# Six merged-head operands loaded ahead of the last projection rows, two of them through ScalarE's queue, and the first dense product written ahead of later casts

## The chip, the cores and the metric

The kernel runs on one core of one Trainium2 chip. Its engines are TensorE (PE, with PEld for its weight loads), VectorE (DVE), ScalarE (ACT), GpSimd (POOL) and SyncE (SP); the last does nothing here but issue DMAs. The metric is the device time of one execution in microseconds, given as the median of the runs.

## The reference

One layer of a streaming encoder on a sequence of 2048 tokens of 1024 features: an attention sub-layer with two groups of eight heads, an output projection of the merged heads, and a squared-ReLU MLP.

```python
def reference(x, c, g_norm1, w_in, g_q, g_k, rel_bias, w_o, g_norm2, w1, w2, w_ada, b_ada):
    ...
        mod = c_act @ w_ada[l] + b_ada[l]
        sh1, sc1, gt1, sh2, sc2, gt2 = [m[:, None, :] for m in jnp.split(mod, 6, axis=-1)]
        h = rmsnorm(x, g_norm1[l]) * (1.0 + sc1) + sh1
        proj = h @ w_in[l]
        q_sb, k_sb, v_sb, q_ca, k_ca, v_ca = jnp.split(proj, split_pts, axis=-1)
        ...
        o_sb = stick_breaking_attention(...)
        ...
        o_ca = chunked_relpos_attention(q_ca, k_ca, hs(v_ca, N_CA_HEADS), rel_bias[l])
        mixed = jnp.concatenate([o_sb.reshape(B, S, D_SB), o_ca.reshape(B, S, D_CA)], axis=-1)
        x = x + gt1 * (mixed @ w_o[l])
        h = rmsnorm(x, g_norm2[l]) * (1.0 + sc2) + sh2
        x = x + gt2 * (jnp.square(jax.nn.relu(h @ w1[l])) @ w2[l])
```

## The kernel before, in words

Everything is computed in float32 by splitting each operand into a high and a low part and multiplying three times (high by high, high by low, low by high): `mm3`. Activations lie transposed, features on the 128 partitions, tokens along the free axis. The tokens are cut into four blocks of 512; the program calls them g or tb, 0 to 3.

The program has four stages. The first projects the input. The second is the attention, head by head, with the remaining projections put between its matmuls. The third is the seam that the change touches. The fourth is the MLP, whose two products are taken apart into seven smaller ones each (the numbers 1, 5, 6, 3, 7, 2, 4 in names such as `ps_0_5` and `opw_0_6`).

At the seam stand, in this order on PE:

- `po_4` to `po_7`: the last four of the eight output projections of token block 1. Each is 24 matmuls of 128x512, of a weight tile `ow_n` (1 MB, one DMA) and eight operands `fx`. The function `row()` writes one of them.
- `pso_5`, `pso_6`, `pso_7`, `pso_0` to `pso_4`: the eight output projections of token block 0 (class `Mixed`), again 24 matmuls each. Their moving operands are `opm_0` to `opm_7`, the merged heads of block 0, loaded by `Mixed.fetch` with eight DMAs of 512 KB from the scratch tensors `scr_m`. `pso_5` to `pso_7` keep the weight tiles `ow_5` to `ow_7` of the rows before; the others have their own, `wo_n`.
- the first dense products of the MLP (class `First`): `ps_0_1`, `ps_0_5`, then those that are added on top in a second PSUM bank, `ps_s`. That bank first gets a copy of `ps_0_1`, made by ACT (`ps_0_1_s`).

The scratch tensors `scr_m_0` to `scr_m_3` of block 0 are stored by SP well before. `scr_m_4` to `scr_m_6` are stored by POOL's queue and `scr_m_7` by ACT's queue; the last three of these come out of the last heads of the attention, while PE is already at `po_4`.

While PE is at the seam, DVE and ACT normalize and split the inputs of the MLP, one of four groups at a time. The first group is loaded into four tiles `ty`, the others into `cy`; `some(k, n)` writes stage n of group k. `txr_n` and `cxr_n` are the residual rows, added by DVE to the finished projections.

What sets the order: each engine executes its instructions in the order in which they stand in the program, a DMA-issuing instruction among them. The recording layer adds the waits. A DMA issued by SP or ACT takes one of eight completion counters, DMAHW0 to DMAHW7, one after the other over both queues, and waits until the DMA that had this counter before it has landed. POOL's DMAs have counters of their own, DMASW0 and so on.

Of the kernel before, what the change touches and what calls it, by code (L numbers as in the profile page):

```python
# [9 lines left out]
F32 = mybir.dt.float32  # L10
# [14 lines left out]
KT = D // P  # L25
# [54 lines left out]
def encoder_kernel(ctx, tc, xs, c, g1, g2, w_in, w_first, w_rest, gqk, bias, w_o, w1, w2, w_ada, b_ada, out):  # L80
    nc = tc.nc
    act, dve, pool, sp = nc.scalar, nc.vector, nc.gpsimd, nc.sync
# [20 lines left out]
    def scratch(name, shape, *counts):  # L103
        return {i: dram.tile(shape, F32, name=name + "_".join(map(str, i))) for i in product(*map(range, counts))}
# [4 lines left out]
    scr_m = scratch("scr_m", [P, 2, TB], NTB, KT)  # L109
# [134 lines left out]
    if True:  # L244
# [251 lines left out]
        act, dve, pool = (Ordered(tc, e) for e in (act, dve, pool))  # L496
# [58 lines left out]
        for i, e in ((0, dve), (KT // 2, pool)):  # L555
            ks = slice(i, i + KT // 2)
# [101 lines left out]
        sp = osp  # L658
# [78 lines left out]
    if True:  # L737
# [7 lines left out]
        sp = nc.sync  # L745
# [262 lines left out]
        class Filler:  # L1008
# [7 lines left out]
            def fetch(self, n):  # L1016

                while len(self.tiles) < n:
                    pl = (hx2, hxp, hxp)[turn[0] % 3]
                    turn[0] += 1  # L1020
                    for k in range(len(self.tiles), len(self.tiles) + KT // 2):
                        t = pl.tile([P, 2, TB], F32R, tag="hx", name=f"fx{turn[0]}_{k}")
                        sp.dma_start(t.bitcast(F32), self.src(k))
                        self.tiles.append(t)
# [332 lines left out]
        steps = [(u, st) for u in units for st in range(STEPS)]  # L1357

        turns = {STEPS * n: 4 if u.ca else 8 for n, u in enumerate(units) if n and u.ca != units[n - 1].ca}
        for i in range(len(steps) + LAG):  # L1360
# [31 lines left out]
            n = len(urgent) + len(heavy)  # L1392
# [14 lines left out]
    sp = osp  # L1407
# [21 lines left out]
    if True:  # L1429
# [35 lines left out]
        steps, jobs = [], {}  # L1465
# [510 lines left out]
        class Mixed(Step):  # L1976
# [6 lines left out]
                self.tiles = 0 if at else KT  # L1983
                self.frees = KT if at == KT - 1 else 0

            def fetch(self, *ks):
                for k in range(*ks):
                    m = Mixed.parts[k] = opp.tile([P, 2, TB], F32R, tag="op", name=f"opm{self.g}_{k}")
                    sp.dma_start(m.bitcast(F32), scr_m[self.g, k])

            def load(self):
                g, n = self.g, self.n
# [98 lines left out]
        def some(k, *ns):  # L2091
            for n in ns:
                blocks[k][n]()
# [3 lines left out]
        def row():  # L2097

            while force(left) is False:
                pass  # L2100
            while len(stores) > 2:
                stores.pop(0)()
            return force(left)

        steps[0].fetch(0, KT // 2)
        row()
        row()
        some(0, 0)
        steps[0].fetch(KT // 2, KT - 2)
        row()  # L2110
        some(0, 1)
        steps[0].fetch(KT - 2, KT)
        row()
        some(0, 2)
        some(1, 0)
# [15 lines left out]
        ahead = iter(steps[1:])  # L2131
        nxt = next(ahead)
        for n, s in enumerate(steps):
            while nxt is not None and ready - used + nxt.tiles <= 8 and nxt.ready():
                nxt.prepare()
                ready += nxt.tiles
                nxt = next(ahead, None)
            for m in (0, 1) if n == 0 else (n + 1,):
                if m < KT:
                    steps[m].load_row()  # L2140
            for job in jobs.get(n, ()):
                job()
            if n == KT - 1:
                firsts = spare.tile([P, 2, 2, TB], F32R, tag="r8", name="opr")
                steps[KT].prepare(firsts[:, 0])
                steps[KT].fetch(0)
                steps[KT + 1].prepare(firsts[:, 1])
                for m in range(1, 4):
                    steps[KT].fetch(m)
            s.run()  # L2150
            used += s.frees
            later.tick()
        later.flush()
# [42 lines left out]
```

## Time and profile before

| | us |
|---|---|
| median of 3 runs | 2514.77 (2513.28 to 2515.25) |
| profiled execution, its time | 2516.38 |
| profiled execution, span of the trace | 2514.6 |
| PE busy | 2498.9 (99%) |
| DVE busy | 2027.7 (81%) |
| ACT busy | 1526.4 (61%) |
| POOL busy | 787.1 (31%) |
| mean granted clock of PE | 0.999 |

The page gives each engine's busy time, and the span in 40 slices of 62.9 us. The timeline lists instructions in order of time, neighbours of a kind merged: start, length, engine, line, operation, output<-inputs, shape, count, and in brackets the idle time ahead of the first with what ended it. Nearly every instruction is recorded by a helper at line 42, so names of tiles tell them apart. SPq and ACTq are the issuing of DMAs; how long one takes to land stands in the answers on a tile.

### The profile page before, as it was taken

The numbers are of one execution on the slowest core, as the hardware profiler recorded it, in microseconds if no ns is written. First come the engines' busy times: TensorE is split into PE (matmuls) and PEld (weight loads), VectorE is DVE, ScalarE is ACT, GpSimd is POOL, SyncE is SP. The second block draws the span as 40 slices with busy tenths as digits, with TensorE's granted clock in tenths as the row PEclk, the third lists the DMA queues.
The fourth block names the chain that finished last, engine by engine and source line by source line (L and its number), as shares of the span: only waits on it lengthen the run. The fifth ranks groups of instructions, "written<-read, shape, count | busy, mean of one in ns | idle before, by whom it ended". The sixth has DMA issues, their size and how long they took to land.

```text
span 2514.6 us, 39505 instructions
## 1 busy us (share of the span) xinstructions
PE 2498.9 (99%) x12364; PEld 2094.8 (83%) x12364; DVE 2027.7 (81%) x3567; ACT 1526.4 (61%) x2928; POOL 787.1 (31%) x1174
## 2 busy tenths in 40 slices
PE   9999999999999999999999999999999999999999
PEld 8888888888888888888888888888888888888887
DVE  7656777897799888999858777779877759799998
ACT  6333424778876686666755555567555546577765
POOL 4330154777776677776710000000000000010100
PEclk9999999999999999999999999999999999999999
DMA  9879978789888788866786878996998996888982
GB/s 357 333 297 362 356 269 291 233 262 311 268 262 260 237 259 254 268 195 216 213 323 245 299 285 305 330 351 191 327 323 269 315 363 262 320 249 282 303 280 84
DMA packets 295970, 704.71 MB, mean 280 GB/s; under 512 B 32080, under 2 KB 88400, under 8 KB 284112
## 3 DMA queue, kind: packets, MB, share of 16 engines
q1 hardware_dynamic: 287552, 684.35, 79.3%
q0 software_dynamic: 6768, 13.11, 2.9%
q10 hardware_dynamic: 1440, 4.72, 0.5%
q8 instruction: 98, 1.61, 0.3%
q14 instruction: 112, 0.92, 0.1%
HBM read 473.99 MB, written 228.07 MB: 279 GB/s over the span
## 4 chain that ended last, share of the span: by engine, by line
PE 86%; DVE 5%; DMA 4%; ACT 2%; issue 1%; POOL 0%; SPq 0%; DVEq 0%; ACTq 0%; POOLq 0%
PE ps L42 24%; PE ps_s L42 15%; PE pt L42 11%; PE acc L42 7%; PE wt L42 7%; PE pf L42 6%; PE z L42 5%; PE po L42 4%; PE pq L42 3%; PE cz L42 2%; PE ct L42 1%; DMA scr_t<-twn 1%; DMA hw<-in_w_dram 1%; DVE h L42 1%; DMA opm<-scr_m 1%
## 5 line engine op out<-in xcount | busy, mean ns | idle before, releaser
L42 ACT CAST wth<-wt 128x512 fp32r<-128x512 f32 (+3 forms) x544 | 257.5, 484 | 173.3 <-PE wt L42 160.7
L42 PE MATMUL ps<-h,opw 128*128 128x512 f32 x1512 | 358.6, 389 | 0.0
L42 POOL TENSOR_TENSOR b<-p 128x512 f32<-128x512 f32 (+1 forms) x320 | 291.9, 912 | 155.7 <-DVE p L42 95.6
L42 DVE TENSOR_TENSOR wtl<-wt,wth 128x512 fp32r<-128x512 f32 (+3 forms) x544 | 291.2, 547 | 60.7 <-ACT wth L42 56.2
L42 PEld LDWEIGHTS ps<-h,opw 128*128 128x128 f32 x1512 | 283.6, 188 | 58.9
L42 PE MATMUL pt<-w,ht 128*128 128x512 f32 x1248 | 288.0, 391 | 0.0
L42 PE MATMUL ps_s<-h,opw 128*128 128x512 f32 x1152 | 277.6, 390 | 1.5 <-ACT ps_s L42 1.0
L42 PEld LDWEIGHTS pt<-w,ht 128*128 128x128 f32 x1248 | 232.9, 188 | 47.5
L42 DVE TENSOR_TENSOR_SCAN p<-z,p,zero 128x512 f32<-128x512 f32 x192 | 245.3, 1279 | 20.6 <-ACT z L42 14.9
L42 PEld LDWEIGHTS ps_s<-h,opw 128*128 128x128 f32 x1152 | 215.7, 188 | 47.9 <-ACT ps_s L42 1.4
L42 ACT CAST opr<-r 128x512 fp32r<-128x512 f32 x280 | 174.3, 623 | 118.2 <-PE ps L42 65.6
L42 PE MATMUL acc<-wth,v 128*128 128x512 f32 (+3 forms) x544 | 221.3, 410 | 1.1 <-ACT o L42 1.1
L42 PE MATMUL ps<-opr,ol 128*128 128x512 f32 x960 | 220.3, 389 | 0.0
L42 PEld LDWEIGHTS ps<-opr,ol 128*128 128x128 f32 x960 | 180.1, 188 | 37.8 <-DVE opr L42 0.4
L42 ACT ACTIVATE z<-z 128x512 f32<-128x512 f32 (+1 forms) x320 | 166.6, 521 | 54.3 <-PE z L42 49.9
L42 DVE TENSOR_TENSOR opr<-r,opr 128x512 fp32r<-128x512 f32 x280 | 185.7, 684 | 13.7 <-ACT opr L42 12.5
L42 PE MATMUL acc<-wtl,v 128*128 128x512 f32 (+3 forms) x544 | 185.6, 347 | 0.0
L42 PE MATMUL z<-k,q 128*128 128x512 f32 (+3 forms) x640 | 182.8, 367 | 1.0 <-DVE p L42 0.9
L42 POOL DMA_DIRECT2D scr_x<-txu x12 | 10.4, 866 | 547.7 <-ACT txu L42 545.9
L42 PE MATMUL ps<-oph,opv 128*128 128x512 f32 x768 | 175.7, 390 | 1.2 <-DVE oph L42 0.9
L42 PE MATMUL wt<-ident,b 128*128 128x128 f32 x1088 | 170.7, 272 | 0.4 <-DVE p L42 0.4
L42 PEld LDWEIGHTS ps<-oph,opv 128*128 128x128 f32 x768 | 143.9, 188 | 32.6 <-DVE oph L42 1.4
(238 smaller groups left out, 5062.1 us busy)
## 6 DMA issues: line engine op xcount, KB each, us to landing
r<-scr_hid SPq DMA_DIRECT2D x80, 512.0 KB, 7.4
q<-scr_q SPq DMA_DIRECT2D x128, 256.0 KB, 5.2
w<-in_w_dram SPq DMA_DIRECT2D x64, 512.0 KB, 5.7
k<-scr_k SPq DMA_DIRECT2D x240, 128.0 KB, 4.6
v<-scr_v SPq DMA_DIRECT2D x120, 256.0 KB, 4.6
wa<-in_w_ada_dram SPq DMA_DIRECT2D x48, 512.0 KB, 6.3
ow<-scr_wo SPq DMA_DIRECT2D x24, 1024.0 KB, 6.7
l<-scr_t SPq DMA_DIRECT2D x20, 1024.0 KB, 8.6
```

The lines of the kernel that those rows point to most:

```text
L42: return lambda *x, **y: self.tc.keep_in_program_order(f(*x, **y))
```

## The change

Three things move; no work is added or taken away.

1. Before, `opm_0` to `opm_3` were fetched ahead of the first row, `opm_4` and `opm_5` behind the second and the `ty` loads, `opm_6` and `opm_7` behind the third. Now `opm_0` to `opm_5` are fetched on SP and `opm_6`, `opm_7` on ACT, all ahead of the first row.
2. `Mixed.fetch` has a parameter for the queue.
3. The product `ps_0_1` (step number KT of the list) is written at the top of its turn, ahead of the preparation of the next five operands, and not behind it.

```diff
-            def fetch(self, *ks):
+            def fetch(self, *ks, queue=sp):
                 for k in range(*ks):
                     m = Mixed.parts[k] = opp.tile([P, 2, TB], F32R, tag="op", name=f"opm{self.g}_{k}")
-                    sp.dma_start(m.bitcast(F32), scr_m[self.g, k])
+                    queue.dma_start(m.bitcast(F32), scr_m[self.g, k])
...
-        steps[0].fetch(0, KT // 2)
+        steps[0].fetch(0, KT - 2)
+        steps[0].fetch(KT - 2, KT, queue=act)
         row()
         row()
         some(0, 0)
-        steps[0].fetch(KT // 2, KT - 2)
         row()
         some(0, 1)
-        steps[0].fetch(KT - 2, KT)
         row()
         some(0, 2)
         some(1, 0)
...
         for n, s in enumerate(steps):
+            if n == KT:
+                s.run()
             while nxt is not None and ready - used + nxt.tiles <= 8 and nxt.ready():
                 nxt.prepare()
...
-            s.run()
+            if n != KT:
+                s.run()
```

The order of PE's and DVE's instructions stays as it was. SP's queue at the seam, with the counters that each DMA waits for. Before:

```order
L42 DMA opm_3_16965<-scr_m_3_163 128x1024 [waits DMAHW4_49]
L42 DMA ow_6_16968<-scr_wo_236 128x2048 [waits DMAHW5_49,PE_49]
L42 DMA txr_5_16970<-in_xs_dram 128x512 [waits DMAHW6_49,Pool_49]
L42 DMA ow_7_16998<-scr_wo_237 128x2048 [waits DMAHW7_49,PE_49]
L42 DMA txr_6_17000<-in_xs_dram 128x512 [waits DMAHW0_49]
L42 DMA ty_0_11_17004<-scr_x_0_216 128x512 [waits DMAHW1_49]
L42 DMA ty_0_12_17006<-scr_x_0_208 128x512 [waits DMAHW2_49]
L42 DMA ty_0_21_17008<-scr_x_4_220 128x512 [waits DMAHW3_49]
L42 DMA ty_0_22_17010<-scr_x_4_212 128x512 [waits DMAHW4_49]
L42 DMA opm_4_17012<-scr_m_4_164 128x1024 [waits DMAHW5_49,DMASW0_49]
L42 DMA opm_5_17014<-scr_m_5_165 128x1024 [waits DMAHW6_49,DMASW1_49]
```

And with the change, the same stretch of SP's queue:

```order
L42 DMA opm_3_16965<-scr_m_3_163 128x1024 [waits DMAHW4_49]
L42 DMA opm_4_16967<-scr_m_4_164 128x1024 [waits DMAHW5_49,DMASW0_49]
L42 DMA opm_5_16969<-scr_m_5_165 128x1024 [waits DMAHW6_49,DMASW1_49]
L42 DMA ow_6_16976<-scr_wo_236 128x2048 [waits DMAHW0_49,PE_49]
L42 DMA txr_5_16978<-in_xs_dram 128x512 [waits DMAHW2_49,Pool_49]
L42 DMA ow_7_17006<-scr_wo_237 128x2048 [waits DMAHW3_49,PE_49]
L42 DMA txr_6_17008<-in_xs_dram 128x512 [waits DMAHW4_49]
L42 DMA ty_0_11_17012<-scr_x_0_216 128x512 [waits DMAHW5_49]
L42 DMA ty_0_12_17014<-scr_x_0_208 128x512 [waits DMAHW6_49]
L42 DMA ty_0_21_17016<-scr_x_4_220 128x512 [waits DMAHW7_49]
L42 DMA ty_0_22_17018<-scr_x_4_212 128x512 [waits DMAHW0_49]
```

`opm_4` and `opm_5` moved ahead of the weights `ow_6` and `ow_7`, and with them the counters moved: the DMA that waits for counter 0 was `txr_6` and is now `ow_6`.

ACT's queue at the end of the attention. Before, the store of the last merged heads, which takes counter 0, is followed by the first group of the MLP's inputs:

```order
L42 DMA scr_m_7_167<-os_7_0_16719 128x1024 [waits DMAHW0_49,Pool_49]
L42 ACTIVATE ty_0_11_17004<-ty_0_11_17004,mod,aff 128x512 [waits DVE_49]
L42 ACTIVATE ty_0_12_17006<-ty_0_12_17006,mod,aff 128x512 [waits DVE_49]
L42 ACTIVATE ty_0_21_17008<-ty_0_21_17008,mod,aff 128x512 [waits DVE_49]
L42 ACTIVATE ty_0_22_17010<-ty_0_22_17010,mod,aff 128x512 [waits DVE_49]
```

With the change, two loads stand between them:

```order
L42 DMA scr_m_7_167<-os_7_0_16719 128x1024 [waits DMAHW0_49,Pool_49]
L42 DMA opm_6_16971<-scr_m_6_166 128x1024 [waits DMAHW5_49,DMAHW3_49,DMAHW6_49,DMAHW2_49,DMAHW7_49,DMAHW1_49,DMASW2_49]
L42 DMA opm_7_16973<-scr_m_7_167 128x1024 [waits DMAHW1_49,DMAHW0_49]
L42 ACTIVATE ty_0_11_17012<-ty_0_11_17012,mod,aff 128x512 [waits DVE_49]
L42 ACTIVATE ty_0_12_17014<-ty_0_12_17014,mod,aff 128x512 [waits DVE_49]
```

`opm_6` waits for POOL's store of `scr_m_6` (DMASW2), `opm_7` for ACT's own store of `scr_m_7` (DMAHW0) to land.

ACT again, at the first dense products (`opw` are casts of the MLP's weights). Before:

```order
L42 CAST opr<-ts_0_1_5_17488 128x512 [waits DVE_49]
L42 CAST opw_0_6_17524<-ts_0_1_6_17492 128x512 [waits DMAHW1_49,DVE_49,PE_49]
L42 CAST opw_0_3_17527<-ts_0_1_3_17494 128x512 [waits DMAHW2_49,DVE_49,PE_49]
L42 CAST opw_0_7_17530<-w_1_0_17441 128x512 [waits DMAHW4_49,DVE_49,PE_49]
L42 CAST opw_0_2_17533<-w_1_0_17441 128x512 [waits PE_49]
L42 CAST opw_0_4_17536<-w_1_0_17441 128x512 [waits DMAHW5_49,PE_49]
L42 COPY ps_0_1_s<-ps_0_1_17539 128x512 [waits PE_49]
```

With the change:

```order
L42 CAST opr<-ts_0_1_5_17488 128x512 [waits DVE_49]
L42 COPY ps_0_1_s<-ps_0_1_17524 128x512 [waits PE_49]
L42 CAST opw_0_6_17539<-ts_0_1_6_17492 128x512 [waits DVE_49]
L42 CAST opw_0_3_17542<-ts_0_1_3_17494 128x512 [waits DMAHW2_49,DVE_49]
L42 CAST opw_0_7_17545<-w_1_0_17441 128x512 [waits DMAHW4_49,DVE_49]
L42 CAST opw_0_2_17548<-w_1_0_17441 128x512
L42 CAST opw_0_4_17551<-w_1_0_17441 128x512 [waits DMAHW5_49]
```

The copy into the second bank moved ahead of the five casts.

## The prediction

> **What bounds the kernel now.** The page comes first.
>
> ```profile
> PE 2498.9 (99%) x12364; PEld 2094.8 (83%) x12364; DVE 2027.7 (81%) x3567; ACT 1526.4 (61%) x2928; POOL 787.1 (31%) x1174
> ```
>
> PE is busy for 99% of the span, so the kernel can gain only where PE stands still, and loses wherever PE is made to stand. The change touches one stretch of about 80 us, so the second view is PE's timeline there.
>
> ```profile
> 1268.66 22.00 PE L42 MATMUL po<-fx,ow 128*128 128x512 f32 x96
> 1290.50 4.29 PE L42 MATMUL pso<-opm,ow 128*128 128x512 f32 x18
> 1296.38 0.96 PE L42 MATMUL pso<-opm,ow 128*128 128x512 f32 x3 [1.59 <-DMA opm<-scr_m]
> 1297.63 11.86 PE L42 MATMUL pso<-opm,ow 128*128 128x512 f32 x51 [0.29 <-DMA opm<-scr_m]
> 1309.33 27.36 PE L42 MATMUL pso<-opm,wo 128*128 128x512 f32 x120
> 1336.53 5.81 PE L42 MATMUL ps<-h,opr 128*128 128x512 f32 x24
> 1343.30 3.04 PE L42 MATMUL ps_s<-h,opw 128*128 128x512 f32 x12 [0.96 <-ACT ps_s L42]
> ```
>
> PE stands still three times: 1.59 and 0.29 us for the late operands opm_6 and opm_7, and 0.96 us for ACT's copy into the second bank. Together 2.84 us, or 0.11% of the run: all that the change can win here. Where it can lose is read from the DMA queue, so the third view is SP's timeline in the same stretch, where each row is an issue and not a transfer.
>
> ```profile
> 1260.72 1.85 SPq L42 DMA_DIRECT2D opm<-scr_m  x4
> 1267.87 0.32 SPq L42 DMA_DIRECT2D ow<-scr_wo  x1
> 1268.28 0.38 SPq L42 DMA_DIRECT2D txr<-in_xs_dram  x1
> 1274.37 0.32 SPq L42 DMA_DIRECT2D ow<-scr_wo  x1
> 1283.85 0.33 SPq L42 DMA_DIRECT2D txr<-in_xs_dram  x1
> 1284.24 1.85 SPq L42 DMA_DIRECT2D ty<-scr_x  x4
> 1286.18 0.85 SPq L42 DMA_DIRECT2D opm<-scr_m  x2
> ```
>
> Between 1274.69 and 1283.85 us SP issues nothing. SP's own list of waits (total, times, longest) names what it waited for,
>
> ```profile
> SPq L42 <- DMA scr_m<-os: 9.1, 1, 9.1
> ```
>
> and the chain that ended last shows how long that transfer took.
>
> ```profile
> 1275.90 7.94 DMA scr_m<-os
> 1283.85 0.33 SPq L42
> ```
>
> The residual row txr_6 took completion counter 0, which ACT's store of scr_m_7 held; issued at 1275.90, that store landed 7.94 us later, and SP's queue stood for 9.1 us. Before, this cost PE almost nothing: both weight tiles that PE needs next, ow_6 and ow_7, were already issued at 1267.87 and 1274.37. It only made opm_6 and opm_7 late.
>
> **The change part by part.** *Loads ahead of the rows.* By the order of the built program, opm_4 and opm_5 now stand ahead of ow_6 and shift the counters by two, and the two loads on ACT take one each as well: ow_6 is now the DMA that waits for counter 0. The store itself does not come earlier, since what makes it is not touched.
>
> ```profile
> 1262.11 0.61 POOL L42 DMA_DIRECT2D scr_m<-os  x1 [0.32 <-POOL os L42]
> 1270.58 0.58 POOL L42 DMA_DIRECT2D scr_m<-os  x1 [0.30 <-POOL os L42]
> 1275.90 0.33 ACTq L42 DMA_DIRECT2D scr_m<-os  x1
> ```
>
> The three rows are the stores of scr_m_5, scr_m_6 and scr_m_7. opm_4 can go at once, at 1262.6 behind opm_3. opm_5 has to wait for the first of them to land, until about 1271; that hides behind the longer wait of ow_6, which starts there.
>
> How long store and weights then take to land is read from the answers on their tiles os and ow. The first two rows are stores of this kind, lightly loaded (at 1227 and 1245 us) and that of scr_m_5, with four loads of 512 KB beside it; the last two are weight tiles, lightly loaded (1207 and 1238 us) and those of the seam.
>
> ```profile
> DMA to landing us min/median/max: 3.9/4.1/4.2
> DMA to landing us min/median/max: 8.5/8.5/8.5
> DMA to landing us min/median/max: 4.7/5.2/5.8
> DMA to landing us min/median/max: 6.7/7.4/8.2
> ```
>
> The store of scr_m_7 had ow_7, 1 MB, issued 1.5 us ahead of it. That load now stands behind the store, so I take the light value, 4.1 us: it lands at 1275.90 + 4.1 = 1280.0, and ow_6 is issued then. The same landing releases opm_7 on ACT's queue, which shares the DMA engines with ow_6, so I take 6.2 us for ow_6, between the light 5.8 and the loaded 6.7: it lands at 1286.2. PE reaches po_6 after po_4 and po_5, which are 48 of the 96 matmuls of the first row: 1268.66 + 11.0 = 1279.7. PE stands for **6.5 us**. The lower end is 3.9 + 4.7, landing at 1284.5, a stall of 4.8; the upper end is 7.9 + 8.2, landing at 1292.0, a stall of 12.3.
>
> po_7 adds nothing: ow_7 follows 0.7 us behind ow_6 with 1 MB more, at the 409 and 420 GB/s of busy stretches (the clock's rows below) some 3 us later, and PE has po_6 to do for 5.5 us. opm_6 and opm_7 land well ahead of pso_5, at 1297, so the **1.88 us** of stalls for them go.
>
> *Two issues on ACT.* opm_7 holds ACT's queue until the store lands, about 1280. What stands behind it is the first scaling of ty.
>
> ```profile
> 1288.47 0.82 ACT L42 ACTIVATE ty<-ty,mod,aff 128x512 f32<-128x512 f32 x1 [13.97 <-DVE ty L42]
> 1287.74 0.69 DVE L42 TENSOR_TENSOR ty<-ty,r 128x512 f32<-128x512 f32 x1 [7.12 <-DMA ty<-scr_x]
> ```
>
> ACT idled 13.97 us there, so a wait of 4 us inside it costs nothing. The ty loads themselves now stand behind ow_6 in SP's queue, the last one behind its landing: issued at about 1286.2 and not by 1286.1, under 2 us later at DVE once the weights ahead of them have moved. DVE and ACT then run their chain at most 2 us late, PE 4 us or more; they have more room than before. DVE's addition of txr_5 waits for a load behind ow_6, until about 1287; behind it stands only ty, not yet there.
>
> *The copy written ahead of the casts.* ACT's rows:
>
> ```profile
> 1339.66 1.35 ACT L42 CAST opw<-ts 128x512 fp32r<-128x512 f32 x2 [1.41 <-PE ps L42]
> 1340.99 1.66 ACT L42 CAST opw<-w 128x512 fp32r<-128x512 f32 x3
> 1342.67 0.57 ACT L42 COPY ps_s<-ps 128x512 f32<-128x512 f32 x1
> ```
>
> Five casts took 3.0 us ahead of the copy. With the copy first it can start when ps_0_1 is done, 12 of the 24 matmuls in 5.81 us, so about 3.0 us behind PE's start there, and end at 3.6; cast and subtraction of opw_6 (about 0.65 us each, half of the 1.35 for two, and as much on DVE) end at about 5.0, and PE wants the second bank behind the 24 matmuls, at 5.5. The **0.96 us** go. A price for the five later casts is bounded by nothing and that same 0.96 us; I take nothing, since four of them are wanted only one product of 2.7 us later each.
>
> *The clock.* A stall of 6.5 us is longer than any of PE's here, and the trace shows one stretch in which PE's granted clock fell. The rows give PE's busy time and count, those of the other engines, and then the granted clock (1.00, 0.59, 0.56, 1.00).
>
> ```profile
> 8.00:12.00 4.00, 3.74 (x32) 3.58 (x32) 3.96 (x6) 2.19 (x4) 0.95 (x1) 1.00 1.05 393
> 12.00:16.00 4.00, 3.87 (x22) 3.58 (x21) 3.12 (x9) 0.61 (x3) 1.61 (x3) 0.59 1.02 409
> 16.00:20.00 4.00, 3.59 (x16) 3.25 (x17) 2.31 (x5) 2.34 (x7) 2.22 (x4) 0.56 1.04 420
> 20.00:24.00 4.00, 4.00 (x19) 3.31 (x18) 3.37 (x7) 3.97 (x10) 4.00 (x4) 1.00 0.67 225
> ```
>
> PE's timeline has at that place:
>
> ```profile
> 10.29 3.09 PE L42 MATMUL pva<-ones,nsqa 128*128 128x1 f32 x24
> ```
>
> After little PE work (24 matmuls of one column from 10.29 on) the clock stood at half, as 0.59 and 0.56 over 8 us make up: (0.41 + 0.44) x 4 / 0.5 = 6.8 us. After the stall of 1.59 us at 1296 it did not fall. An idle of 6.5 us is nearer to the former. Its price is between nothing and half of 6.8 us, 3.4; part of a half-rate stretch may lie in the stall itself, so I take **2.0 us**.
>
> [...]
>
> **The sum.** 6.5 + 2.0 - 1.88 - 0.96 = +5.7 us. The profiled execution has a span of 2514.6 us, so 2520.3 for that; its time of 2516.38 is 1.6 us above the median of the runs, to which I add the same: 2514.77 + 5.7 = **2520.4 us**, 0.23% slower. After the seam PE waits almost nowhere, so what is lost is not caught up. By the ends: 4.8 + 0 - 2.84 = +2.0, and 12.3 + 3.4 - 2.84 = +12.9.
>
> **The rivals.** *The light case, no difference that can be told.* A measurement of this kernel can tell about 0.2%, 5.0 us, from no change. If stall and clock together stay under 7.9 us, the result is within that. The clock holding decides it: 6.5 - 2.84 = +3.7, 2518.4 us. For it speaks that no clock fell in any stall of the trace after the start; against it, that none was over 1.6 us. Light transfers do the same: 8.6 us in place of 10.3, a stall of 4.8 and 1.5 for the clock, +3.5.
>
> [...]
>
> *The slow case.* If the store lands as late as before, at 1283.84, and ow_6 takes the 8.2 us of its neighbour, +10 to +12.9, 2524.8 to 2527.7. For it speaks that two of the stores in the rows took about 8 us; against it, that those had 1 to 2 MB of loads beside them.
>
> *The change does what it says, and is not slower.* The weights' wait hides, the three stalls go, 2514.77 - 2.84 = 2511.9 us, still within 0.2%. It decides when ow_6 lands by 1279.7, or, to break even, by 1282.5. That needs 6.6 us for store and weights in a row; the shortest rows make 8.6. Only an earlier store would do, and nothing here moves it.
>
> **How the numbers follow.** Forecast, +5.0 to +8: 0.52. Slow case, above +8: 0.14. Light case, +2 to +5: 0.30. The stalls gone and the wait hidden, -2.8 to +2: 0.03; anything faster by over 5.0 us needs a mechanism that I don't see: 0.01. So slower by over 0.2%: 0.66; within: 0.33; faster: 0.01. The range leaves out about a tenth on either side: 2517.0 (the light case's lower end) to 2525.5.
>
> **What would show it.** PE's timeline should have one new idle of 5 to 8 us ahead of the 49th of the 96 po matmuls, put down to the DMA ow<-scr_wo or to its issue, and the rows with 1.59, 0.29 and 0.96 should be gone. SP's waits should still have one of about 9 us for scr_m<-os, now in front of an ow. The granted clock in the 7 us after po_6 starts should show about half if the clock's term is right, with matmuls twice as far apart. I am wrong if ow_6 is issued ahead of the store's landing, or if PE passes from po_5 to po_6 without a gap.

## The result, and the profile after

The changed kernel takes 2519.37 us (median of 11 runs, 2517.92 to 2520.84), the kernel before, run beside it, 2514.0 us (11 runs, 2511.59 to 2516.01): a ratio of 1.0022, with a 95% interval of 1.0015 to 1.003. It is 5.4 us slower. The forecast was 2520.4 us, 0.23% slower.

The profiled execution of the changed kernel has a time of 2518.76 and a span of 2517.1 us. Against the span of 2514.6 before that is only 2.5 us, less than half of what the medians show; the profiled execution of before was 2.4 us above its median. That is taken up with the last experiment.

PE's timeline at the seam (start, length, what, count, and the idle time ahead with what ended it):

```profile
1267.90 11.12 PE L42 MATMUL po<-fx,ow 128*128 128x512 f32 x48
1285.53 12.52 PE L42 MATMUL po<-fx,ow 128*128 128x512 f32 x48 [6.51 <-DMA ow<-scr_wo]
1297.88 16.48 PE L42 MATMUL pso<-opm,ow 128*128 128x512 f32 x72
...
1341.40 5.60 PE L42 MATMUL ps<-h,opr 128*128 128x512 f32 x24
1346.84 2.88 PE L42 MATMUL ps_s<-h,opw 128*128 128x512 f32 x12
```

The three idle times of before (1.59, 0.29, 0.96) are gone, and there is one of 6.51 us ahead of the 49th po matmul, `po_6`. Behind it the 48 matmuls of `po_6` and `po_7` take 12.52 us, where the 48 of `po_4` and `po_5` ahead of it took 11.12.

SP's timeline, ACT's two rows of issues, and SP's list of waits (total, times, longest) say why `ow_6` came late:

```profile
1259.96 11.01 SPq L42 DMA_DIRECT2D opm<-scr_m  x6
1277.89 0.32 SPq L42 DMA_DIRECT2D ow<-scr_wo  x1
1278.79 0.38 SPq L42 DMA_DIRECT2D ow<-scr_wo  x1
...
1275.13 0.33 ACTq L42 DMA_DIRECT2D scr_m<-os  x1
1276.27 1.92 ACTq L42 DMA_DIRECT2D opm<-scr_m  x2
...
SPq L42 <- DMA scr_m<-os: 15.1, 2, 8.3
```

SP waits twice for a store of scr_m. The first wait, the longest of 8.3 us, lies inside the 11.01 us of the six opm (`opm_5`, until the store of scr_m_5 has landed). The second, 15.1 - 8.3 = 6.8 us, ends ahead of `ow_6`, which goes out at 1277.89. The answers on the tiles os and ow give that store's landing and the landing of `ow_6`:

```profile
DMA to landing us min/median/max: 2.7/2.7/2.7
DMA to landing us min/median/max: 7.5/7.5/7.5
```

1275.13 + 2.7 = 1277.8, and `ow_6` is issued; 1277.89 + 7.5 = 1285.4, and PE goes on. Stretches of PE and the granted clock (behind the stretch stands its length, then PE's busy time and in brackets its matmuls; the clock is the 1.00 or 0.50 near the end):

```profile
1278.19:1281.60 3.41, 0.83 (x4) 0.37 (x2) 0.00 (x0) 0.00 (x0) 0.00 (x0) 1.00 0.83 288
1281.60:1285.01 3.41, 0.00 (x0) 0.00 (x0) 0.00 (x0) 0.00 (x0) 0.00 (x0) 0.50 0.98 365
1285.01:1288.43 3.42, 2.90 (x7) 2.38 (x8) 0.75 (x1) 0.00 (x0) 0.00 (x0) 0.50 0.99 377
1288.43:1291.84 3.41, 3.41 (x17) 2.79 (x16) 1.29 (x2) 0.60 (x1) 0.00 (x0) 1.00 1.04 371
```

The clock stands at half from 1281.60 to 1288.43, 6.8 us; 2.9 us of that lie behind the restart at 1285.53 and cost half of themselves, 1.4 us. That is the 12.52 - 11.12.

### The profile page after: what moved, and what is told of

It reads as the page before. It is cut to its first block, busy times and chain, and to the rows that moved or that the text cites. A ratio compares the mean times of both kernels' runs of the same rounds, so it can differ in the third digit from the quotient of the medians.

```text
span 2517.1 us, 39506 instructions
## 1 busy us (share of the span) xinstructions
PE 2496.6 (99%) x12364; PEld 2094.5 (83%) x12364; DVE 2027.5 (81%) x3567; ACT 1526.1 (61%) x2928; POOL 787.6 (31%) x1174
## 3 DMA queue, kind: packets, MB, share of 16 engines
q8 instruction: 98, 1.61, 0.3%
## 4 chain that ended last, share of the span: by engine, by line
PE 91%; DVE 3%; DMA 3%; ACT 2%; issue 1%; POOL 0%; SPq 0%; DVEq 0%; ACTq 0%; POOLq 0%
PE ps L42 25%; PE ps_s L42 16%; PE pt L42 11%; PE acc L42 8%; PE wt L42 7%; PE pf L42 6%; PE z L42 5%; PE po L42 5%; PE pq L42 3%; PE cz L42 2%; PE pso L42 2%; PE ct L42 1%; DMA hw<-in_w_dram 1%; PE px L42 1%; DVE opv L42 0%
## 5 line engine op out<-in xcount | busy, mean ns | idle before, releaser
L42 PEld LDWEIGHTS ps_s<-h,opw 128*128 128x128 f32 x1152 | 215.9, 188 | 45.6 <-DVE cp L42 0.7
```

Source lines behind the costliest of these rows:

```text
L42: return lambda *x, **y: self.tc.keep_in_program_order(f(*x, **y))
```

## The experiments

Beside the idle times, one measure is used throughout: where PE is, counted from its first `po_4` matmul of the seam (1268.66 in the profile of before, 1267.90 in that of the changed kernel). It is worked out from the starts in PE's timeline of each profile.

| us from the start of po_4 | po_6 | pso_5 | pso_0 | first ps_s | second ps_s | end of PE | median of the runs |
|---|---|---|---|---|---|---|---|
| before (its four profiles) | 11.0 | 21.8 | 39.5 to 42.7 | 73.6 to 75.3 | 79.3 to 81.4 | 1239.8 to 1242.5 | 2514.0 to 2515.4 |
| the change (three) | 16.6 to 19.8 | 29.2 to 33.3 | 45.6 to 49.6 | 78.2 to 82.3 | 83.6 to 87.7 | 1242.7 to 1247.0 | 2519.37, 2519.91 |
| copy_only | 11.0 | 21.8 | 42.2 | 74.9 | 80.7 | 1241.1 | 2514.81 |
| loads_only | 18.2 | 31.0 | 47.3 | 80.0 | 85.4 | 1246.1 | 2520.35 |
| six_sp | 10.9 | 23.5 | 39.8 | 73.1 | 80.1 | 1240.3 | 2515.8 |
| four_act | 11.0 | 21.8 | 40.6 | 76.7 | 83.5 | 1244.9 | 2519.26 |
| all_sp | 19.2 | 32.9 | 49.2 | 81.9 | 87.3 | 1246.6 | 2520.28 |
| warm | 18.3 | 29.2 | 45.6 | 78.2 | 84.5 | 1243.8 | 2517.69 |
| pool_two | 11.0 | 21.8 | 38.6 | 73.8 | 80.7 | 1241.0 | 2516.07 |

Diffs are against the changed kernel.

### Which DMA stands behind the store: six_sp

```diff
         steps[0].fetch(0, KT - 2)
-        steps[0].fetch(KT - 2, KT, queue=act)
         row()
...
         some(0, 1)
+        steps[0].fetch(KT - 2, KT)
         row()
```

> opm_4 and opm_5 stay ahead of the first row on SP, opm_6 and opm_7 go back to SP behind the third row. By the built program's counters ow_6 now takes counter 7, which an old load had, and txr_5, behind it, takes counter 0, so that SP's wait for the store of scr_m_7 moves one DMA further back. My theory (the counter decides which load waits for the store): ow_6 is issued at about 1271, right behind opm_5, lands near 1278 to 1279 and PE passes to po_6 with an idle under 1 us; the wait for scr_m<-os is at txr_5, ow_7 is issued at about 1278.3 and lands between 1284 and 1287, while PE wants it at about 1284.5: a stall of 0 to 2.5 us ahead of po_7 (the 73rd of the 96). No clock falls. Against before: -2.8 to +1, so 3 to 8 us faster than the kernel with the whole change. Rival (the place behind opm_4 and opm_5 is what makes the weights late, whoever holds counter 0): a stall of 5 us or more ahead of po_6, and a time like that of the whole change, +5.

Measured: 2515.8 us (11 runs), ratio to before 1.0004 (0.9995 to 1.0013). SP's and PE's timelines:

```profile
1271.74 0.49 SPq L42 DMA_DIRECT2D ow<-scr_wo  x1
1280.88 0.33 SPq L42 DMA_DIRECT2D txr<-in_xs_dram  x1
...
1268.74 16.61 PE L42 MATMUL po<-fx,ow 128*128 128x512 f32 x72
1286.66 5.73 PE L42 MATMUL po<-fx,ow 128*128 128x512 f32 x24 [1.32 <-DMA ow<-scr_wo]
```

`ow_6` goes out at 1271.74 with `opm_4` and `opm_5` still ahead of it, and PE passes into `po_6` and through it without a gap; the wait for the store stands one DMA further on, at `txr_5`, and costs 1.32 us ahead of `po_7`, within the 0 to 2.5 expected. No clock falls. So it is the counter, shifted by ACT's two loads, that put `ow_6` behind the store. Not met was the time, "-2.8 to +1" against before: the median is 1.6 us above the 2514.16 of before, with an interval from -1.3 to +3.3. PE is 1.6 us earlier than in the first profile of before at the first ps_s, but only 0.2 us earlier at the second. PE's timeline there, and ACT's rows ahead of what it waits for:

```profile
1348.79 3.03 PE L42 MATMUL ps_s<-h,opw 128*128 128x512 f32 x12 [1.40 <-ACT cp L42]
...
1345.38 0.62 ACT L42 CAST opw<-w 128x512 fp32r<-128x512 f32 x1 [2.44 <-DMA w<-in_w_dram]
1347.63 0.62 ACT L42 CAST opw<-ts 128x512 fp32r<-128x512 f32 x1 [1.64 <-DVE ts L42]
1348.16 0.58 ACT L42 COPY cp<-ps_s 128x512 f32<-128x512 f32 x1
```

The copy `cp` that frees the second bank stands on ACT behind casts that wait for the MLP's weights `w` and for DVE's `ts`. It comes at about 80 us however early PE is: wherever `ow_6` and `ty` are on time, the second ps_s starts at 79.3 to 81.4 us, with the three stalls of before or without them. What the change meant to win at the seam had another wait right behind it. An earlier load of `w` was not tried.

### Is it ACT's queue: all_sp

```diff
-        steps[0].fetch(0, KT - 2)
-        steps[0].fetch(KT - 2, KT, queue=act)
+        steps[0].fetch(0, KT)
         row()
```

> All eight opm on SP ahead of the first row, none on ACT. By the counters opm_7 takes counter 0 and ow_6, behind it, counter 1. SP takes its DMAs in order, so ow_6 still stands behind the landing of the store of scr_m_7, by the data that opm_7 needs. My theory (standing behind that landing on SP is what costs, not ACT's two issues): ow_6 is issued at about 1278, lands at 1285 to 1286 with opm_7 beside it, PE idles 6 to 7.5 us ahead of po_6 and the clock falls: +4.5 to +7 against before, within 1 us of the whole change. Rival (the two loads on ACT's queue are what slows the weights or holds ACT's work): the stall is 4.5 us or less and the time +3 or less.

Measured: 2520.28 us (9 runs), ratio 1.0025 (1.0015 to 1.0034).

```profile
1287.46 13.92 PE L42 MATMUL po<-fx,ow 128*128 128x512 f32 x48 [8.03 <-DMA ow<-scr_wo]
```

The stall is there without any load on ACT, 8.03 us, half a microsecond longer than expected, and the time is that of the whole change. For `ow_6` to stand behind the landing of scr_m_7 on SP, by a counter or by SP's order, is enough. What the two loads on ACT cost by themselves this run doesn't tell, since more than they changed: the store of scr_m_7 took 5.4 us here and not 2.7, `ow_6` went out at 1281.42, 3.4 us later than expected, and then took 5.9 us and not 7.5.

### ACT's queue with nothing behind the store on SP: four_act

```diff
-        steps[0].fetch(0, KT - 2)
-        steps[0].fetch(KT - 2, KT, queue=act)
+        steps[0].fetch(0, KT // 2)
+        steps[0].fetch(KT // 2, KT, queue=act)
```

> opm_0 to opm_3 on SP as before, opm_4 to opm_7 on ACT's queue, behind its store of scr_m_7; the early copy stays. By the counters nothing that PE needs waits for that store on SP: ow_6 takes counter 6, ow_7 counter 3, and counter 0 is taken by opm_6 on ACT. My theory: ow_6 and ow_7 go out at about 1268 and 1275 as before, PE has no idle ahead of po_6, the wait for scr_m<-os shows on ACT's queue, where ACT idles anyway; opm_6 and opm_7 are issued at about 1278 and land by 1287, ahead of pso_5 at 1290.5, so that the stalls of 1.59, 0.29 and 0.96 us go: -2 to -3.3 us against before, -7 to -9 against the whole change. Rival (four loads of 512 KB started together on ACT's queue take the DMA engines from ow_7 and ty): a new stall of 1 us or more at po_7, pso_5 or ps_0_1, and no gain against before.

Measured: 2519.26 us (11 runs), ratio 1.0018 (1.0009 to 1.0027): as slow as the whole change, against an expected gain of 2 to 3.3. PE's timeline, SP's and its list of waits:

```profile
1268.21 22.00 PE L42 MATMUL po<-fx,ow 128*128 128x512 f32 x96
1290.06 16.48 PE L42 MATMUL pso<-opm,ow 128*128 128x512 f32 x72
1308.84 29.08 PE L42 MATMUL pso<-opm,wo 128*128 128x512 f32 x120 [2.30 <-DMA wo<-scr_wo]
...
1274.30 0.54 SPq L42 DMA_DIRECT2D txr<-in_xs_dram  x1
1284.77 5.58 SPq L42 DMA_DIRECT2D ty<-scr_x  x4
...
SPq L42 <- DMA opm<-scr_m: 16.7, 5, 9.9
```

The first half of the theory held: no idle ahead of `po_6`, `po_7` or within pso_5 to pso_7. But I had followed the counters only for what PE needs. The counters that `opm_4`, `opm_5` and `opm_6` hold on ACT are those that three of the four `ty` loads on SP take next, so SP stood for 9.9 us ahead of the first `ty` and issued the last one at 1290. Everything behind them in SP's queue came late, the first `wo` to begin with (2.30 us ahead of pso_0, and then 29.08 us for the 120 matmuls that took 27.36 before, as half the clock for 3.4 us makes it); DVE's and ACT's chain, which starts from `ty`, came late too, with waits of 0.36 and 0.74 us ahead of ps_0_1 and of 1.25 us at the second ps_s. The rival was right that `ty` would come late and that nothing would be gained; the one stall of over 1 us before the second ps_s came at pso_0, which it didn't name, and its reason (bandwidth) was not needed.

### The early product alone, and the loads alone: copy_only, loads_only

copy_only has the loads as before and the early product; loads_only has this:

```diff
         for n, s in enumerate(steps):
-            if n == KT:
-                s.run()
...
-            if n != KT:
-                s.run()
+            s.run()
```

> The loads stand as before; only the product ps_0_1 is written ahead of the preparation of the later operands. My theory: the stalls of 1.59 and 0.29 us for opm_6 and opm_7 stay, the idle of 0.96 us in front of the first ps_s matmul goes or shrinks below 0.2: -0.5 to -1.3 us, within 0.2%. Rival (the five casts behind the copy are now late for ps_s): an idle of 0.3 us or more at ps_s with a cast of opw as its cause, and a time 0 to +1.

> The loads as in the whole change, the product ps_0_1 written where it was. My theory: the stall of about 6.5 us ahead of po_6 is there as with the whole change, and the granted clock falls to half behind it; since PE reaches ps_0_1 some 5 us later and ACT does its casts no later, the copy is waited for by 0.96 us or less. Time against before: +4.5 to +7, no more than 1 us from the whole change. Rival (the early product itself costs time further on): the time comes out at +3 or less, with the stall ahead of po_6 still there.

Measured: copy_only 2514.81 us (11 runs), ratio 1.0003 (0.9994 to 1.0012); loads_only 2520.35 us (11 runs), ratio 1.0023 (1.0015 to 1.0032). PE's timeline of loads_only:

```profile
1287.12 12.94 PE L42 MATMUL po<-fx,ow 128*128 128x512 f32 x48 [7.11 <-DMA ow<-scr_wo]
...
1343.42 5.60 PE L42 MATMUL ps<-h,opr 128*128 128x512 f32 x24
1348.86 2.88 PE L42 MATMUL ps_s<-h,opw 128*128 128x512 f32 x12
```

The loads alone make the loss. And the idle of 0.96 us ahead of ps_s is gone in loads_only as well, without the early product: PE comes 5 us later or more, and the copy is in time wherever it stands. In copy_only the idle is gone too, but two of its rows show what came instead:

```profile
1296.27 13.48 PE L42 MATMUL pso<-opm,ow 128*128 128x512 f32 x51 [0.29 <-DMA opm<-scr_m]
...
1348.09 3.01 PE L42 MATMUL ps_s<-h,opw 128*128 128x512 f32 x12 [0.26 <-ACT cp L42]
```

The 51 matmuls that took 11.86 us in the first profile of before took 13.48 here: the clock fell to half for 3.4 us behind the stall for `opm_6` (1296.41 to 1299.82). PE was thus late at the first ps_s in any case, and the profile does not show what the early product is worth alone. The times do: nothing that can be told, 0.65 us more than before where 0.5 to 1.3 less was expected.

### The stall without the fall of the clock: warm and after_again

```diff
         row()
         row()
+        warm = pz.tile([P, TB], F32, tag="z", name="warm", bufs=4)
+        keep_busy(25, warm)
         some(0, 0)
```

> The whole change, and 25 extra matmuls of 128x128 between po_5 and po_6 into a tile that nothing reads: work added, the result of the kernel untouched. They fill the start of the stall. My theory (the half-rate stretch behind the stall is caused by PE's idling): the weights still come when they come, so po_6 starts within 0.3 us of the whole change's, the granted clock stays at 1.00 behind it if the remaining idle is short (under 4 us), and the run is 1 to 1.8 us shorter than the whole change, +3.5 to +4.5 against before. Rival (the clock falls for another reason, or costs nothing, or the extra matmuls outlast the stall): the same time as the whole change, or more.

> The whole change once more, beside the two kernels above, so that they are compared on the same chip: +4 to +7 us against before, a stall of 6 to 7 us ahead of po_6 and half the clock for 6.8 us behind it. A rival that the stall's length is a matter of one profile: 4.5 us or less, or 8 or more.

Measured: warm 2517.69 us (11 runs), ratio 1.0015 (1.0006 to 1.0024); the whole change beside it 2519.91 us (9 runs), ratio 1.0026 (1.0016 to 1.0035). PE's timeline of warm, and of the whole change in this profile:

```profile
1274.30 5.75 PE L42 MATMUL warm<-ones 128*128 128x128 f32 x50
...
1286.82 11.13 PE L42 MATMUL po<-fx,ow 128*128 128x512 f32 x48 [1.55 <-DMA ow<-scr_wo]
...
1285.33 12.77 PE L42 MATMUL po<-fx,ow 128*128 128x512 f32 x48 [5.50 <-DMA ow<-scr_wo]
```

The extra matmuls came out as 50 and stood behind the 25th po matmul and not between po_5 and po_6; they took 5.5 us, and what was left of the stall was 1.55. The clock did not fall, and the 48 matmuls took 11.13 us, not 12.77: the fall behind the stall costs 1.6 us here, and it went with PE's idling. An idle near the 4 us of the expectation was not tried, and behind one of 1.61 us in before_again the clock did fall. The medians differ by 2.2 us, more than the 1 to 1.8 expected, with intervals that overlap. In the profiles themselves the gain is hidden, since `ow_6` landed later against po_4 in that of warm (po_6 at 18.3 us and not at 16.6).

### The operands through a queue with counters of its own: pool_two

```diff
-        steps[0].fetch(0, KT - 2)
-        steps[0].fetch(KT - 2, KT, queue=act)
+        steps[0].fetch(0, KT // 2)
+        steps[0].fetch(KT - 2, KT, queue=pool)
         row()
         row()
         some(0, 0)
+        steps[0].fetch(KT // 2, KT - 2)
```

> opm_0 to opm_5 on SP where they stood before, opm_6 and opm_7 through POOL's queue, which has counters of its own; the early copy stays. SP's queue and its counters are then those of before: txr_6 waits for the store of scr_m_7, and ow_6 and ow_7 go out ahead of it. POOL has nothing to do at the seam behind its last product at 1274.58. My theory (the counters that ACT's two loads take are what costs, not the wish to have opm_6 and opm_7 earlier): no idle ahead of po_6 or po_7; opm_6 is issued at about 1276.5 and opm_7 at about 1284, landing near 1283 and 1291 to 1292, ahead of their use at 1294.6 and 1295.3; the stalls of 1.59 and 0.29 us go, and so does the half clock that such a stall brought in copy_only; the early copy brings 0.7. Against before -2 to -4 us. Rival (POOL's loads take the DMA engines from opm_4, opm_5 and ty, as four loads on ACT's queue held ty back): a stall of 1 us or more at pso_5 or pso_0, and no gain.

Measured: 2516.07 us (11 runs), ratio 1.0005 (0.9996 to 1.0014). PE's timeline:

```profile
1268.78 22.00 PE L42 MATMUL po<-fx,ow 128*128 128x512 f32 x96
1290.61 16.88 PE L42 MATMUL pso<-opm,ow 128*128 128x512 f32 x72
...
1335.99 0.73 PE L42 MATMUL ps<-h,opr 128*128 128x512 f32 x2 [0.94 <-ACT opr L42]
1337.46 5.29 PE L42 MATMUL ps<-h,opr 128*128 128x512 f32 x22 [0.74 <-DVE opr L42]
...
1349.51 3.03 PE L42 MATMUL ps_s<-h,opw 128*128 128x512 f32 x12 [1.32 <-ACT cp L42]
```

This does what the change set out to do: no idle ahead of po_6 or po_7, none over 0.2 us in pso, and PE is at pso_0 at 38.6 us, 1.0 to 4.1 us earlier than in any profile of before. Then it waits 0.94 and 0.74 us for the first operands of the MLP and 1.32 for `cp`, and is at the second ps_s at 80.7 us, inside the range of before. That fits the theory that the counters make the loss. But `opm_4` and `opm_5` also stand behind `ow_6` and `ow_7` again here, so it is six_sp that parts the counter from the place. The gain of 2 to 4 us did not come, because PE waits for ACT and DVE right behind. Part of that may be POOL's doing, as the rival had it, only further on: `opm_7` goes out at 1284.03, just ahead of the first `ty`, which took 5.2 us to land and not 3.5. That `ty` landed 20.5 us behind po_4 (18.0 to 19.5 in before), and ACT's first cast of `opr` began at 66.6 (65.3 to 67.0). How much of the 0.94 and 0.74 us comes from that was not tested. No version tried beats the kernel before.

### How much single executions differ: before_again, before_p3, before_p4, after_p3

No edit: three more profiles of the kernel before and one of the changed kernel.

> The kernel before once more, with a profile: ratio 1.000 within 0.1%. From the first matmul of po_4 to the end of PE's work the profile shown took 1241.57 us. If part of the loss is given back behind the seam, this one takes about the same, 1241 to 1242; if the profile shown of before is only a long one by chance, as its time of 2516.38 against the median suggests, 1239 to 1240.5, and the loss is then the whole difference of the seam. The stalls of about 1.59, 0.29 and 0.96 us are there again; whether the clock falls behind the first of them is open.

> The kernel before, a third profile. Open is why the two profiles of it (1241.57 and 1242.47 us from po_4 to the end of PE's work) stand only 1 to 3 us below those of the whole change (1244.74 and 1242.72), where the medians of the runs differ by 5.4 to 5.9. If that is chance in single executions, a profile whose time is near the median, 2514 to 2515, takes 1239.5 to 1240.5 here and shows less waiting or no fall of the clock in the seam. If part of the loss is given back behind the seam, it takes 1241 or more whatever its time, and what it is shorter by lies ahead of po_4.

> The same, a fourth profile: by chance in single executions its time and its stretch from po_4 to the end go together, about 1239.5 to 1240.5 for a time of 2514 to 2515; given back, 1241 or more. Behind the stall for opm_6 the clock falls in some profiles and not in others, and costs about 1.6 us where it does.

> The whole change, a third profile: a stall of 5.5 to 7.1 us ahead of po_6, half the clock for 6.8 us behind it, 48 matmuls from po_6 on in 12.5 to 12.9 us and not 11.1. From po_4 to the end 1242.5 to 1246 us by chance in single executions, and with a time near 2519.5 about 1244 to 1245.5.

Measured: before_again 2515.41 us (10 runs), ratio 1.0002 (0.9993 to 1.0011). The profiled executions of before took 2516.38, 2517.89, 2514.86 and 2514.43 us, and from po_4 to the end 1241.6, 1242.5, 1239.8 and 1240.1; those of the changed kernel 2518.76, 2517.58 and 2521.67, and 1244.7, 1242.7 and 1247.0. Time and stretch go together, and near its median the kernel before takes about 1240: the two spans that stood only 2.5 us apart were a long execution of before beside a middling one of the changed kernel. before_again was a long one again and decided nothing; it also lacked the expected 0.96 us ahead of ps_s, since PE was late there after a fall of the clock (half from 1299.20 to 1302.61). The stall ahead of po_6 differs most. It was expected at 6 to 7 us in after_again and at 5.5 to 7.1 in after_p3, and was 5.50 (the row above) and 8.64:

```profile
1288.24 13.72 PE L42 MATMUL po<-fx,ow 128*128 128x512 f32 x48 [8.64 <-DMA ow<-scr_wo]
```

There the clock stood at half for 10.2 us (1283.47 to 1293.71) and not 6.8, and the stretch from po_4 to the end was above the 1246 us expected at most.

Something seems to be given back all the same. By the means of the four and the three profiles the changed kernel is 5.1 us behind at the second ps_s (85.24 - 80.12) and 3.8 at the end (1244.83 - 1241.00). Of the 1.3 us, 0.5 come back in the first 300 us behind the seam, in every pair of profiles (298.0 to 298.4 us from the second ps_s to the first matmul of `oph`, the MLP's second product, against 297.6 to 297.8). The other 0.8 lie further on and are not shown. PE of before waits there for DVE (`cp`, `oph`, `txo`) 1.1 to 1.6 us in all, PE of the changed kernel 0.2 to 1.1. But loads_only, where PE is as late, waits 1.6 us there, and takes 1160.7 us from the second ps_s to the end, as long as before (1160.3 to 1161.3). Two of the four executions of before were also longer than all its medians.

## Why the prediction was right, point by point

- *The counter.* Right: `ow_6` waits for counter 0 and goes out at the store's landing; SP's wait for it in front of `ow_6` was 6.8 us, not about 9: the longer one, 8.3 us, is that of `opm_5`. six_sp moved the counter and the stall went.
- *Stall, 6.5 us.* Measured 6.51, 5.50 and 8.64 in the three profiles, 6.9 in the mean. That the first agrees to 0.01 is luck: both of its parts were mis-sized, and the errors cancel. The store took 2.7 us, less than the light value of 4.1 and under the lower end of 3.9; `ow_6` took 7.5, not 6.2, with `opm_7` started in the same moment. Their sum of 10.2 stands against the 10.3 of the forecast. Over the three profiles the store took 2.7 to 3.1 us and `ow_6` 6.4 to 9.3: it is the load that makes the spread.
- *po_7 adds nothing.* Right: the 48 matmuls stand in one row.
- *Clock, 2.0 us.* The mechanism is right. By the rows for 48 matmuls it cost 1.4, 1.65 and 2.6 us, and 1.8 and 2.8 in loads_only and all_sp. One of its reasons, "After the stall of 1.59 us at 1296 it did not fall", holds for that one profile only: behind a stall of 1.61 and 1.54 us it did fall in before_again and copy_only (below).
- *-1.88 us for opm_6 and opm_7.* Both idle times went. But the kernel before has them at 1.88, 1.86, 0.90 and 0.79 us in its four profiles, and in one of them half the clock behind, 1.6 us more; 1.8 in the mean, so the term's size holds by these idle times. They count from the modelled end of a matmul; by the starts, the way from pso_5 to pso_0 takes 18.8 us in the mean of before and 16.3 with the change, 2.5 less.
- *-0.96 us for the copy.* It went. The copy does come 2.9 us behind PE's start, as the step has it, but this wasn't needed: loads_only shows that PE's lateness alone is enough. Where PE is not late, the early copy does remove the idle, and the next wait on ACT takes it back (1.40 us in six_sp, 1.32 in pool_two).
- *ACT held by opm_7 costs nothing; DVE and ACT at most 2 us late.* The first is right: ACT's `ty` waited 17.51 us, for DVE. The second was exceeded. ACT's first scaling of `ty` is at 1291.24, which is 23.3 us behind po_4 and was 19.8, so 3.5 late; but PE was 8.1 us late at pso_5, and ACT waits for PE 4.14 us ahead of the copy where it waited 1.41.
- *"What is lost is not caught up."* Not quite: 0.5 us come back in every pair of profiles, and perhaps 0.8 more, which the runs don't show. "After the seam PE waits almost nowhere" was read as nothing to win back, though PE of before waits there for DVE 1.1 to 1.6 us.
- *The rivals.* The light and the slow case are ends of one mechanism's spread, not alternatives to it: the stalls of 5.50 and 8.64 us lie between the 4.8 and the 12.3 of these two. The slow case's condition, a store that lands as late as before, was met in none of the three profiles. "The change does what it says", -2.84 us, had its price wrong: pool_two took the stalls away without the new one, and nothing was won. I had not asked there what is late next.
- *The total.* Forecast +5.7, measured +5.4. The mechanism carries it; that it fits to 0.3 us is partly luck, with profiled executions of the changed kernel 4 us apart.

## What to carry to other kernels

Here the DMAs of SP and ACT take eight completion counters in turn, and the four loads that moved shifted which later DMA waits for which earlier one: SP's wait for the store of scr_m_7 went from `txr_6` (9.1 us, in the profile of before) to `ow_6` (6.8), and in four_act SP stood 9.9 us ahead of the first `ty`. With such counters, list counter and holder for every DMA from the edit on, through everything PE needs and everything the helping engines need. When a stall is to be removed, look at what the next engine can deliver at that moment; here the copy `cp` came at about 80 us however early PE was. A difference of 5 us that hangs on how long single DMAs take wants several profiles of both kernels, since one pair showed half of it.

## What the runs showed of the hardware

The clock's changes lie on a grid in these traces. By their records of the clock, the stretches at half rate are 6.827 us long in the first profile of before, 3.413 and 6.827 in that of the changed kernel, and three rows of 3.41 to 3.42 in after_p3: one, two or three steps of 3.413 us. Those of one execution start a whole number of such steps apart (in the changed kernel 15.25 and 1281.60 us, 371 steps of 3.4133), and the stretch at full rate behind the half-rate one in before is 2495.143 us, 731 steps. Cut along that grid, the steps of PE behind the stall for opm_6 in copy_only and in the first profile of before, and behind the stall in warm:

```profile
1292.99:1296.41 3.42, 1.59 (x7) 0.68 (x6) 3.42 (x7) 1.26 (x3) 0.00 (x0) 1.00 1.03 413
1296.41:1299.82 3.41, 3.41 (x9) 2.67 (x10) 3.33 (x6) 1.24 (x2) 0.00 (x0) 0.50 1.05 404
...
1292.72:1296.13 3.41, 2.07 (x9) 1.25 (x8) 2.98 (x5) 2.06 (x4) 0.00 (x0) 1.00 1.04 415
1296.13:1299.55 3.42, 2.88 (x11) 2.10 (x12) 3.42 (x7) 1.45 (x3) 0.00 (x0) 1.00 1.04 404
...
1283.63:1287.04 3.41, 1.85 (x9) 1.27 (x8) 0.00 (x0) 0.00 (x0) 0.00 (x0) 1.00 1.00 380
1287.04:1290.45 3.41, 3.41 (x16) 2.82 (x16) 0.75 (x1) 0.00 (x0) 0.00 (x0) 1.00 0.99 375
```

In copy_only the stalls of 1.54 and 0.29 us fall into one step, PE is busy for 1.59 us of it, and the next step is at half clock. In before the 1.59 and 0.29 us are cut by a step's border, PE is busy for 2.07 and 2.88 us, and the clock stays at 1.00. In the seam, at full clock, it fell behind steps with 0.00 us of work (after_p3), 0.83 (the changed kernel), 1.55 (before_again) and 1.59 (copy_only), and held behind those with 1.85 (warm), 2.07 and 2.88 (before). These are steps of matmuls of 512 columns: at the start of the run, in the first profile of before, PE was busy for 3.36 us of the step from 9.30 to 12.72, with 24 of its 31 matmuls one column wide, and the next step was at half all the same. What is counted is left open. So behind the stalls of 1.54 and 1.61 us in copy_only and before_again the 51 matmuls took 1.6 us more (13.48 and 13.47 against 11.86), and behind the 1.59 of before no more, by where the stall fell on the grid.

Rising took more here than holding: in after_p3, at half clock, a step with 2.05 us of work was followed by another at half, where at full clock 1.85 us had been enough to hold in warm. In all_sp the 48 matmuls behind the stall took 13.92 us and not 11.12, which makes 5.6 us of them at half, more than one step. (In the changed kernel's own rows above, one with 2.90 us was followed by full clock; at the start of the run, in the first profile of before, one with 3.28 us, from 12.72 on, by another at half.)

```profile
1286.88:1290.29 3.41, 2.05 (x5) 1.69 (x6) 0.75 (x1) 0.00 (x0) 0.00 (x0) 0.50 1.00 390
1290.29:1293.71 3.42, 3.42 (x9) 2.65 (x9) 1.35 (x3) 0.62 (x1) 0.00 (x0) 0.50 1.05 405
```

And in these runs the time of a store went with what was issued just ahead of it. The store of scr_m_7, 512 KB, landed after 7.9 us in before, with a load of 1 MB issued 1.5 us ahead of it, and after 2.7, 2.9 and 3.1 us in the changed kernel, with that load behind it. All runs agree: 6.7 to 8.1 us in the seven profiles with that load 1.5 us ahead, 4.8 with a load of 1 MB 4.2 us ahead (six_sp), 5.4 with a load of 512 KB 0.2 us ahead (all_sp), and 2.8 in loads_only and warm, which have it behind.
